# RWKV A products on the 64 rows of one head, the two heads by turns

## The chip, the core and the metric

The kernel runs on one core of a Trainium2 chip. A core has five engines with an instruction queue each: TensorE (PE in the profile, its weight loads PEld), VectorE (DVE), ScalarE (ACT), GpSimd (POOL) and SyncE (SP). Each queue runs in order, and semaphores make one queue wait for another. The metric is the device time of one execution in microseconds (us), lower is better; before, it is 991.96, the median of three runs.

## The reference

One step of a one-layer model: RWKV-7 time mixing and a differential attention on the same normalised input, gates, and an MLP. 512 prompt tokens and 64 sample tokens (8 sequences of 8) run together as 576 columns. The change lies in the RWKV part, eight heads of 64 channels:

```python
def rwkv7_scan(S0, r, w, k, v, a, b):
    ...
    def step(S, inp):
        r_t, w_t, k_t, v_t, a_t, b_t = inp
        sa = jnp.einsum('bhij,bhj->bhi', S, a_t)
        S = S * w_t[:, :, None, :] + sa[..., None] * b_t[:, :, None, :] + v_t[..., None] * k_t[:, :, None, :]
        return S, jnp.einsum('bhij,bhj->bhi', S, r_t)
...
    S, y = rwkv7_scan(S0, hs(r), hs(decay), hs(k), hs(v), -kk, kk * hs(a))
```

## The kernel before

**Chunks.** The scan is computed in nine chunks of 64 tokens, eight of the prompt and one of the samples (chunk 8). Within a chunk the steps become matrix products and a triangular inverse. The eight heads are handled as four pairs, `hp` 0 to 3; a pair fills the 128 partitions, head `par` 0 in rows 0 to 63, head `par` 1 in rows 64 to 127.

**`rwkv(hp)`** is a generator that prepares a pair, in stages that end at each `yield`. The first stage makes the tiles of keys and queries: `KB` has on the rows of each head, for each chunk, 64 columns of `b` and 64 of `k`; `ST0` and `ST1`, one for each head, have on the rows of their own head 64 columns of `a` and 64 of `r`, and zeros on the other 64 rows, put there by a memset on GpSimd (line 819). Then come the products called `pA`: for each head and each chunk `KB` (128 x 128) against that head's `ST` (128 x 128), with sums over 128 rows, of which 64 are zero. Groups of 4, 4 and 1 chunks write one PSUM bank each, named by pair, head and first chunk: `pA108` is pair 1, head 0, chunk 8. VectorE evicts a bank in two halves with a mask: the head's own rows of the result go to `ABR`, the other rows go into the zero half of `ST`, where they serve as the second operand of the scan.

The second stage transposes the values (`pV`, evicted by ScalarE into `SVU`) and `KB` (`pK`, into `KBt`), and multiplies the states of the samples with `ST` on 64 x 64 corners, the heads by turns (`pI`, copied by ScalarE into chunk 8 of `ST`). The third stage inverts the triangular part: ScalarE copies four pieces of 32 rows of `ABR`, two of each head, into `DT`; VectorE makes `Y` and the transposed `X` of it; TensorE multiplies 32 x 32 blocks (`pW`, `pZ`), in several rounds.

**`chain(pr)`** runs the scan over the chunks for two pairs at once, with the short products `pch`.

**Work beside it.** The projections of the input through the weights are the bulk of the work: `stream` yields one 128 x 128 by 128 x 288 product after another (`psz`, `psg` by name `ps_z`, `ps_g`; `gg` and `tz` are their evictions), and `take(n)` and `fill(n)` put n of them between the steps of the RWKV part. The calls `run(0, 0)`, `take(221)`, `run(0, 1, 1)` and so on at the end set in which order the stages of the pairs are written.

**What sets the order.** The tile framework's scheduler turns this into one queue for each engine, by priorities and by its own estimate of when an operand is ready; projections have the lowest priority (`FILL`), weight loads and evictions the highest (`FEED`). The order is fixed when the kernel is built. `bank(...)` gives one of three PSUM banks, which `pA`, `pV`, `pK`, `pI` and others share by turns; a bank is given anew when its evictions have ended. All products are in f32 with fp32r halves for the projections; helper `mm` is line 72, `tr` line 76, `act` line 58, `tt` line 61, so the profile's rows are told apart by their tiles.

Of the kernel before, what the change touches and what calls it, by code (L numbers as in the profile page):

```python
# [15 lines left out]
P = 128  # L16
# [20 lines left out]
C_ID, C_OB, C_M, C_MS, C_LM, C_I32, C_HS, C_SEL, C_MB, C_CM, C_END = (  # L37
    0, 128, 256, 384, 512, 672, 704, 706, 738, 746, 748)
# [3 lines left out]
def tile_hybrid_step(ctx, tc, xT, xsT, ktab, vtab, s0T, ptab, w_in, vecs, w2a2, g2, lamv,  # L42
# [3 lines left out]
    PE, VE, AE, GE = nc.tensor, nc.vector, nc.scalar, nc.gpsimd  # L46
# [13 lines left out]
    def tt(out, a, b, op, eng=None):  # L60
        ins = (eng or VE).tensor_tensor(out=out, in0=a, in1=b, op=op)  # L61
        if eng is None:
            ring["tt"] = ins

    def stt(out, a, s, b, op0, op1):
        VE.scalar_tensor_tensor(out=out, in0=a, scalar=s, in1=b, op0=op0, op1=op1)
# [4 lines left out]
    def mm(out, lhsT, rhs, start=True, stop=True):  # L71
        ring["mm"] = PE.matmul(out=out, lhsT=lhsT, rhs=rhs, start=start, stop=stop)  # L72
        return ring["mm"]
# [27 lines left out]
    def bank(name):  # L101
        return psw.tile([P, 512], F32, tag="w", name=name)
# [616 lines left out]
    def ch(a):  # L719
        return a.rearrange("p (c t) -> p c t", t=64)  # L720

    def m3(ap_, n):
        q, w = ap_.shape
        return ap_.rearrange("p (o w) -> p o w", o=1).broadcast_to([q, n, w])
# [15 lines left out]
    halves = [(par, slice(64 * par, 64 * par + 64)) for par in range(2)]  # L740

    def rwkv(hp):
        e = hp % 2
        own = pair.setdefault(hp // 2, {})
# [17 lines left out]
        nb = rt.tile([P, 5, P], F32, tag="G", name=f"nb{hp}", bufs=3)  # L762
# [50 lines left out]
        ST = []  # L813
        for par, rows in halves:
            stt(KB[rows, :, par], ch(aa)[rows], 0.5, ch(pinv)[rows], MUL, MUL)
            tt(KB[rows, :, 1 - par], ch(k2)[rows], ch(pinv)[rows], MUL)
            st = rb_.tile([P, NCH, 2, 64], F32, tag=f"ST{par}", name=f"ST{par}_{hp}")
            with tc.issue_after(own["nb"].ins) if hp == 0 else nullcontext():
                GE.memset(st[64 - 64 * par:128 - 64 * par], 0.0)
            stt(st[rows, :, 0], ch(kk)[rows], -1.0, ch(pm)[rows], MUL, MUL)  # L820
            tt(st[rows, :, 1], ch(r)[rows], ch(pe)[rows], MUL)
            ST.append(st)
        KBc = [KB[:, ci].rearrange("p a t -> p (a t)") for ci in range(NCH)]


        ABR = rb_.tile([P, NCH, 2, 64], F32, tag="ABR", name=f"ABR{hp}")
        for par in range(2):
            rows = slice(64 * par, 64 * par + 64)
            oth = slice(64 - 64 * par, 128 - 64 * par)
            for c0, cn, mk in ((0, 4, C_M), (4, 4, C_M), (8, 1, C_MS)):  # L830
                pA = bank(f"pA{hp}{par}{c0}")
                for i in range(cn):
                    mm(pA[:, i * P:(i + 1) * P], KBc[c0 + i], ST[par][:, c0 + i])
                pAv = pA[:, :cn * P].rearrange("p (c w) -> p c w", c=cn)
                f2 = lambda a: a[:, c0:c0 + cn].rearrange("p c a t -> p c (a t)")
                tt(f2(ABR)[rows], pAv[rows], m3(c[rows, mk:mk + P], cn), MUL)
                tt(f2(ST[par])[oth], pAv[oth], m3(c[oth, mk:mk + P], cn), MUL)
# [29 lines left out]
        for par in range(2):  # L867
            rows = slice(64 * par, 64 * par + 64)
# [202 lines left out]


    gens = [rwkv(hp) for hp in range(4)]

    def run(*stages):
# [249 lines left out]
    rows = []  # L1325
# [10 lines left out]
    for t0, n in LAST:  # L1336
# [63 lines left out]
        for d in range(KT):  # L1400
# [4 lines left out]
            if d + 1 in ends:  # L1405
                i = ends.index(d + 1)
# [119 lines left out]
```

## Time and profile before

| | |
|---|---|
| time, median of 3 runs (lowest, highest) | 991.96 us (991.02, 992.61) |
| profiled execution: time, span | 993.35 us, 991.6 us |
| mean granted TensorE clock | 0.989 |
| busy TensorE, its weight loads, VectorE, ScalarE, GpSimd | 97%, 92%, 70%, 50%, 9% |

The span runs from the first instruction to the last. Busy time by stretch, in us, with the granted clock:

| stretch | what is in it | TensorE | VectorE | ScalarE | clock |
|---|---|---|---|---|---|
| 180 to 206 | pair 0: `pA` to `pI` | 24.19 | 23.59 | 11.06 | 1.00 |
| 206 to 262 | pair 0: inverse; pair 1: tiles | 55.40 | 36.24 | 23.93 | 0.97 |
| 262 to 285 | pair 1: `pA` to inverse | 21.38 | 18.14 | 10.36 | 0.93 |
| 285 to 350 | scan of pairs 0 and 1; pair 2: tiles | 62.85 | 40.78 | 27.20 | 1.00 |
| 350 to 380 | pair 2: `pA` on; pair 3: tiles | 28.82 | 24.57 | 16.91 | 0.94 |
| 380 to 420 | pair 3: `pA` to inverse | 38.52 | 26.37 | 19.43 | 1.00 |
| 420 to 500 | scan of pairs 2 and 3, gates | 76.79 | 45.11 | 31.59 | 1.00 |
| 500 to 991.6 | output projections and MLP | 481.96 | 352.75 | 247.08 | 0.99 |

A row of a group of instructions gives line, engine, operation, output tile <- input tiles, the rows and columns of the array in use (128\*128), the tile's shape and type and the count; then busy time in us, mean ns of one, and the idle time just before them with what ended most of it. In rows in order of time, the first two numbers are start and duration in us, and square brackets hold a wait ahead of the row and what ended it. A product in f32 leaves two records.

### The profile page before, as it was taken

To read this page: it belongs to the slowest core of one execution; us is meant where nothing else is said; L and a number is where in the kernel's file an instruction comes from. 1 tells how busy PE (TensorE), PEld (TensorE's weight loads), DVE (VectorE), ACT (ScalarE), POOL (GpSimd) and SP (SyncE) were. 2 spreads that over 40 slices of the span, in tenths; PEclk is the share of its full clock that TensorE was granted. 3 is DMA by queue.
4 is the path that set the end of the run, shared out by engine and by line. 5 is a ranking of instruction groups with operands and counts; after the bars stand their busy time and mean duration, and the time that the engine had idled before them with its cause. 6 is when DMAs were issued, how large, how long until landed. Compare 5 with 4: busy or idle time off the path is not lost.

```text
span 991.6 us, 24377 instructions
## 1 busy us (share of the span) xinstructions
PE 964.5 (97%) x9996; PEld 913.4 (92%) x9996; DVE 694.3 (70%) x1459; ACT 495.1 (50%) x1084; POOL 91.0 (9%) x171
## 2 busy tenths in 40 slices
PE   8999999999999998999999999999999999999996
PEld 8999989898986898988889999999999999999996
DVE  6698566874945779445688898966666666666744
ACT  6576455354344455443344767444444444444732
POOL 2611100401003230001200000000000000000001
PEclk9999999999999999999999999999999999999998
DMA  7322673221112215222377642222222222221402
GB/s 266 128 76 76 210 220 117 80 59 52 44 63 74 79 62 161 79 70 100 121 234 223 209 132 97 87 94 86 86 86 86 85 86 86 86 87 42 136 3 95
DMA packets 50832, 105.73 MB, mean 107 GB/s; under 512 B 6066, under 2 KB 8114, under 8 KB 50594
## 3 DMA queue, kind: packets, MB, share of 16 engines
q1 hardware_dynamic: 47442, 96.95, 30.4%
q0 software_dynamic: 1648, 5.35, 1.5%
q8 instruction: 78, 1.28, 0.6%
q10 hardware_dynamic: 1632, 1.89, 0.5%
q14 instruction: 32, 0.26, 0.1%
HBM read 89.38 MB, written 14.78 MB: 105 GB/s over the span
## 4 chain that ended last, share of the span: by engine, by line
PE 83%; DVE 6%; issue 6%; ACT 3%; POOL 1%; DMA 0%; SPq 0%; DVEq 0%; POOLq 0%; ACTq 0%
PE ps_dn L72 21%; PE ps_z L72 8%; PE ps_g L72 7%; PE ux L1250 5%; PE ua L1250 5%; PE ps_wo L72 4%; PE ps_brb L72 3%; PE ps_k L72 3%; PE ub L1250 3%; PE ud L1250 3%; PE ps_bra L72 3%; PE uc L1250 3%; PE pch L1010 2%; PE ps_q L72 2%; PE ps_v L72 2%
## 5 line engine op out<-in xcount | busy, mean ns | idle before, releaser
L72 PE MATMUL ps_dn<-q,hi_dn 128*128 128x288 f32 x768 | 154.7, 296 | 0.0
L72 PEld LDWEIGHTS ps_dn<-q,hi_dn 128*128 128x128 f32 x768 | 122.9, 188 | 1.4
L72 PE MATMUL ps_dn<-q,lo_dn 128*128 128x288 f32 x384 | 113.3, 295 | 0.0
L72 PE MATMUL ps_g<-xl,hi_g 128*128 128x288 f32 x256 | 79.7, 311 | 0.0
L72 PE MATMUL ps_g<-xh,lo_g 128*128 128x288 f32 x256 | 79.2, 309 | 0.0
L72 PE MATMUL ps_g<-xh,hi_g 128*128 128x288 f32 x256 | 78.5, 307 | 0.0
L72 PEld LDWEIGHTS ps_dn<-q,lo_dn 128*128 128x128 f32 x384 | 72.2, 188 | 0.0
L72 PE MATMUL ps_z<-xh,lo_z 128*128 128x288 f32 (+1 forms) x224 | 69.2, 310 | 0.0
L72 PE MATMUL ps_z<-xh,hi_z 128*128 128x288 f32 (+1 forms) x224 | 68.0, 303 | 0.0
L72 PE MATMUL ps_z<-xl,hi_z 128*128 128x288 f32 (+1 forms) x224 | 66.9, 299 | 0.0
L61 DVE TENSOR_TENSOR ya<-ya,ps_dn 128x288 f32<-128x288 f32 x96 | 43.3, 451 | 27.6 <-PE ps_dn L72 27.5
L58 ACT ACTIVATE hi_dn<-raw_dn 128x512 fp32r<-128x512 f32 x48 | 30.1, 628 | 56.2 <-PE ps_dn L72 56.1
L58 ACT ACTIVATE c<-c 128x288 f32<-128x288 f32 x112 | 48.8, 440 | 9.4 <-DVE c L61 7.7
L1250 PE MATMUL ux<-h_t,hi 128*128 128x288 f32 x256 | 52.4, 297 | 0.0
L1250 PE MATMUL ua<-h_b,hi 128*128 128x288 f32 x256 | 52.2, 296 | 0.0
L72 PEld LDWEIGHTS ps_g<-xl,hi_g 128*128 128x128 f32 x256 | 48.9, 191 | 1.5
L72 PEld LDWEIGHTS ps_g<-xh,lo_g 128*128 128x128 f32 x256 | 49.0, 191 | 1.3
L72 PEld LDWEIGHTS ps_g<-xh,hi_g 128*128 128x128 f32 x256 | 48.8, 191 | 1.0
L58 ACT ACTIVATE hi<-a 128x1024 fp32r<-128x1024 f32 (+1 forms) x32 | 27.1, 846 | 43.1 <-PE ps_dn L72 34.9
L61 DVE TENSOR_TENSOR lo<-s,hi 128x1024 fp32r<-128x1024 f32 x32 | 39.2, 1224 | 10.4 <-ACT hi L58 10.3
L72 PE MATMUL ps_dn<-q,w 128*128 128x320 f32 (+1 forms) x336 | 46.3, 298 | 0.0
L72 PEld LDWEIGHTS ps_dn<-q,w 128*128 128x128 f32 x336 | 45.3, 190 | 0.1
(391 smaller groups left out, 2789.1 us busy)
## 6 DMA issues: line engine op xcount, KB each, us to landing
a<-in_w_up_dram SPq DMA_DIRECT2D x32, 512.0 KB, 3.3
raw_dn<-in_w_down_dram SPq DMA_DIRECT2D x64, 256.0 KB, 2.8
raw_g<-in_w_in_dram SPq DMA_DIRECT2D x32, 256.0 KB, 3.0
raw_z<-in_w_in_dram SPq DMA_DIRECT2D x28, 256.0 KB, 3.1
gt_d<-gg SPq DMA_DIRECT2D x16, 288.0 KB, 2.3
g<-gt_d SPq DMA_DIRECT2D x16, 288.0 KB, 3.6
kp<-in_ktab_dram SPq DMA_DIRECT2D x16, 256.0 KB, 4.0
vp<-in_vtab_dram SPq DMA_DIRECT2D x16, 256.0 KB, 3.4
```

What stands on the lines that cost most here:

```text
L58: ring["act"] = AE.activation(out=out, in_=in_, func=func, **kw)
L61: ins = (eng or VE).tensor_tensor(out=out, in0=a, in1=b, op=op)
L72: ring["mm"] = PE.matmul(out=out, lhsT=lhsT, rhs=rhs, start=start, stop=stop)
L1010: ring["mm"] = PE.matmul(out=ps[rows, e], lhsT=lhs, rhs=rhs, start=first and e == 1, stop=True, skip_group_check=True)
L1250: ring["mm"] = PE.matmul(out=ps[:, :288], lhsT=l[:, k], rhs=hb[blk][:, h, k], start=start and i == 0, stop=i == 11, skip_group_check=skip)
```

## The change

The products use only the rows of their head: `KB` and `ST` are cut to `[rows]`, 64 of the 128 rows of the array. The loop over the groups of chunks is now outside the loop over the heads: for each group two banks are taken, one for each head, and the products of the two heads are written by turns, one from the one half of the array's rows, the next from the other. Then both banks are evicted. The memset of the other half goes away; the evictions write there before anything reads it.

```diff
--- before.py
+++ after.py
@@ -815,8 +815,6 @@
             stt(KB[rows, :, par], ch(aa)[rows], 0.5, ch(pinv)[rows], MUL, MUL)
             tt(KB[rows, :, 1 - par], ch(k2)[rows], ch(pinv)[rows], MUL)
             st = rb_.tile([P, NCH, 2, 64], F32, tag=f"ST{par}", name=f"ST{par}_{hp}")
-            with tc.issue_after(own["nb"].ins) if hp == 0 else nullcontext():
-                GE.memset(st[64 - 64 * par:128 - 64 * par], 0.0)
             stt(st[rows, :, 0], ch(kk)[rows], -1.0, ch(pm)[rows], MUL, MUL)
             tt(st[rows, :, 1], ch(r)[rows], ch(pe)[rows], MUL)
             ST.append(st)
@@ -824,13 +822,16 @@
 
 
         ABR = rb_.tile([P, NCH, 2, 64], F32, tag="ABR", name=f"ABR{hp}")
-        for par in range(2):
-            rows = slice(64 * par, 64 * par + 64)
-            oth = slice(64 - 64 * par, 128 - 64 * par)
-            for c0, cn, mk in ((0, 4, C_M), (4, 4, C_M), (8, 1, C_MS)):
+        for c0, cn, mk in ((0, 4, C_M), (4, 4, C_M), (8, 1, C_MS)):
+            pAs = []
+            for par in range(2):
                 pA = bank(f"pA{hp}{par}{c0}")
-                for i in range(cn):
-                    mm(pA[:, i * P:(i + 1) * P], KBc[c0 + i], ST[par][:, c0 + i])
+                pAs.append(pA)
+            for i in range(cn):
+                for (par, rows), pA in zip(halves, pAs):
+                    mm(pA[:, i * P:(i + 1) * P], KBc[c0 + i][rows], ST[par][rows, c0 + i])
+            for (par, rows), pA in zip(halves, pAs):
+                oth = halves[1 - par][1]
                 pAv = pA[:, :cn * P].rearrange("p (c w) -> p c w", c=cn)
                 f2 = lambda a: a[:, c0:c0 + cn].rearrange("p c a t -> p c (a t)")
                 tt(f2(ABR)[rows], pAv[rows], m3(c[rows, mk:mk + P], cn), MUL)
```

`halves` is the list of (`par`, `rows`) of both heads.

On TensorE, around pair 0's products (`ps_z9` is a projection). Before:

```order
L72 MATMUL ps_z9_0_3032<-xl_104,hi_z9_1_3028 128x288
L72 MATMUL pA000_2825<-ST0_0_2814,KB0_2810 128x128 x4
L72 MATMUL pA004_2832<-ST0_0_2814,KB0_2810 128x128 x4
L72 MATMUL pA008_2839<-ST0_0_2814,KB0_2810 128x128
L72 MATMUL ps_z9_0_3032<-xh_103,lo_z9_1_3029 128x288
L72 MATMUL ps_z9_0_3032<-xh_103,hi_z9_1_3028 128x288
L72 MATMUL ps_z9_0_3032<-xl_104,hi_z9_1_3028 128x288
L72 MATMUL ps_z9_0_3032<-xh_103,lo_z9_1_3029 128x288
L72 MATMUL pA010_2843<-ST1_0_2820,KB0_2810 128x128 x4
L72 MATMUL ps_z9_0_3032<-xh_103,hi_z9_1_3028 128x288
```

and in the changed kernel:

```order
L72 MATMUL ps_z9_0_3030<-xl_104,hi_z9_1_3026 128x288
L72 MATMUL pA010_2824<-ST1_0_2819,KB0_2810 128x128 x4
L72 MATMUL pA004_2837<-ST0_0_2814,KB0_2810 128x128 x2
L72 MATMUL pA014_2838<-ST1_0_2819,KB0_2810 128x128 x2
L72 MATMUL pA004_2837<-ST0_0_2814,KB0_2810 128x128
L72 MATMUL pA014_2838<-ST1_0_2819,KB0_2810 128x128
L72 MATMUL pA004_2837<-ST0_0_2814,KB0_2810 128x128
L72 MATMUL pA014_2838<-ST1_0_2819,KB0_2810 128x128
L72 MATMUL pA008_2851<-ST0_0_2814,KB0_2810 128x128
L72 MATMUL ps_z9_0_3030<-xh_103,lo_z9_1_3027 128x288
```

The groups of 4 of the two heads now stand next to each other; head 1's first four stand before everything of the second group, whose rows alternate by twos and ones (head 0's first four stand further up, head 1's last further down, both between projections).

On TensorE around pair 1's first groups (`ps_z11`, `ps_g8` are projections). Before:

```order
L72 MATMUL ps_z11_1_3994<-xh_103,lo_z11_1_3990 128x296
L72 MATMUL pA104_3847<-ST0_1_3829,KB1_3825 128x128 x4
L72 MATMUL ps_g8_0_4064<-xh_103,hi_g8_0_4056 128x288
L72 MATMUL ps_g8_0_4064<-xl_104,hi_g8_0_4056 128x288
L72 MATMUL ps_g8_0_4064<-xh_103,lo_g8_0_4057 128x288
L72 MATMUL pA108_3854<-ST0_1_3829,KB1_3825 128x128
L72 MATMUL ps_g8_0_4064<-xh_103,hi_g8_0_4056 128x288
L72 MATMUL ps_g8_0_4064<-xl_104,hi_g8_0_4056 128x288
L72 MATMUL ps_g8_0_4064<-xh_103,lo_g8_0_4057 128x288
L72 MATMUL ps_g8_0_4064<-xh_103,hi_g8_0_4056 128x288
```

and in the changed kernel:

```order
L72 MATMUL ps_z11_1_3990<-xh_103,lo_z11_1_3986 128x296
L72 MATMUL pA110_3837<-ST1_1_3832,KB1_3823 128x128 x4
L72 MATMUL ps_g8_0_4060<-xh_103,hi_g8_0_4052 128x288
L72 MATMUL ps_g8_0_4060<-xl_104,hi_g8_0_4052 128x288
L72 MATMUL ps_g8_0_4060<-xh_103,lo_g8_0_4053 128x288
L72 MATMUL pA104_3850<-ST0_1_3827,KB1_3823 128x128 x4
L72 MATMUL ps_g8_0_4060<-xh_103,hi_g8_0_4052 128x288
L72 MATMUL ps_g8_0_4060<-xl_104,hi_g8_0_4052 128x288
L72 MATMUL ps_g8_0_4060<-xh_103,lo_g8_0_4053 128x288
L72 MATMUL ps_g8_0_4060<-xh_103,hi_g8_0_4052 128x288
```

Before, the three groups of head 0 stood first, those of head 1 fourteen rows later; now head 1's first group comes second. Each group of pair 1 still stands between projections.

On ScalarE in pair 1, from the copies into `DT` to those from `pI` and, in the changed kernel, the first round of the inverse (`W1_1`); `gg8` and `tz11` are evictions of projections. Before:

```order
L58 ACTIVATE DT1_4095<-ABR1_3839 32x288 x2
L58 ACTIVATE SVU0_2861<-pV1_0_3876 64x4x64 x2
L58 ACTIVATE gg8_4051<-gg8_4051 128x288
L58 ACTIVATE SVU0_2861<-pV1_0_3876 64x4x64 x2
L58 ACTIVATE DT1_4095<-ABR1_3839 32x288
L58 ACTIVATE SVU0_2861<-pV1_448_3885 64x64 x2
L58 ACTIVATE DT1_4095<-ABR1_3839 32x288
L58 ACTIVATE KBt1_3889<-pK10_3890 128x512
L58 ACTIVATE KBt1_3889<-pK14_3896 128x512
L58 ACTIVATE KBt1_3889<-pK18_3902 128x128
L58 ACTIVATE tz11_4045<-Z11_3979,vec_73 128x585
L58 ACTIVATE ST0_1_3829<-pI1_3915 64x64 x2
```

and in the changed kernel:

```order
L58 ACTIVATE gg8_4047<-gg8_4047 128x288
L58 ACTIVATE SVU0_2859<-pV1_0_3872 64x4x64 x4
L58 ACTIVATE SVU0_2859<-pV1_448_3881 64x64 x2
L58 ACTIVATE DT1_4091<-ABR1_3835 32x288
L58 ACTIVATE KBt1_3885<-pK10_3886 128x512
L58 ACTIVATE KBt1_3885<-pK14_3892 128x512
L58 ACTIVATE KBt1_3885<-pK18_3898 128x128
L58 ACTIVATE tz11_4041<-Z11_3975,vec_73 128x585
L58 ACTIVATE ST0_1_3827<-pI1_3911 64x64 x2
L58 ACTIVATE ST1_1_3832<-pI1_3911 64x64 x2
L58 ACTIVATE DT1_4091<-ABR1_3835 32x288 x3
L58 ACTIVATE W1_1_4104<-pW11_4105 128x288
```

The four copies into `DT` stood apart, all of them ahead of the copies from `pI`; now one stands ahead of them and three behind.

## The prediction

> **What bounds the kernel now.** I read the page first: the busy times and the chain that ended last.
>
> ```profile
> PE 964.5 (97%) x9996; PEld 913.4 (92%) x9996; DVE 694.3 (70%) x1459; ACT 495.1 (50%) x1084; POOL 91.0 (9%) x171
> PE 83%; DVE 6%; issue 6%; ACT 3%; POOL 1%; DMA 0%; SPq 0%; DVEq 0%; POOLq 0%; ACTq 0%
> ```
>
> TensorE is the bound: 97% busy, 83% of the chain. Its queue runs in the order written, so a microsecond that TensorE loses anywhere is lost at the end, unless it was about to wait there anyway. Then the groups of instructions, shapes kept apart:
>
> ```profile
> L72 PE MATMUL pA<-ST,KB 128*128 128x128 f32 x144 | 19.2, 280 | 0.3
> L61 DVE TENSOR_TENSOR ABR<-pA,cst_sb 64x512 f32<-64x512 f32 x16 | 11.0, 685 | 0.9 <-PE pA L72 0.6
> L819 POOL MEMSET ST<- 64x1152 f32 x8 | 8.4, 1056 | 24.1 <-PE pch L1010 23.8
> ```
>
> The 72 A products leave 144 records, two for each product in f32. A bank of four products is evicted by two VectorE instructions of 0.69 us. The eight memsets go away; GpSimd is 9% busy and no TensorE row names the memset as what it waited for, so I count their 8.4 us as nothing. What could lose that cover is VectorE's write of the next `ST`, which waits for the same buffer with or without them.
>
> **The price of a product now.** The order of time on TensorE where the first head pair's products stand:
>
> ```profile
> 194.72 2.23 PE L72 MATMUL pA<-ST,KB 128*128 128x128 f32 x18
> 196.70 0.38 PE L72 MATMUL ps_z<-xh,lo_z 128*128 128x288 f32 x1
> 196.92 0.29 PE L72 MATMUL ps_z<-xh,hi_z 128*128 128x288 f32 x1
> 197.05 0.30 PE L72 MATMUL ps_z<-xl,hi_z 128*128 128x288 f32 x1
> ```
>
> Eighteen records take 196.70 - 194.72 = 1.98 us: 0.11 a record, 0.22 a product, 72 x 0.22 = 15.9 us in all. The projections beside them follow one another every 0.13 us.
>
> **What a 64-row product can gain.** No row shows 64 rows by 128 columns in two halves by turns. The nearest is `pI`, two heads by turns on 64x64 corners:
>
> ```profile
> 205.24 1.11 PE L72 MATMUL pI<-ST,s 64*64 64x16 f32 x32 [0.35 <-ACT KBt L58]
> 206.28 0.41 PE L72 MATMUL ps_z<-xh,hi_z 128*128 128x296 f32 x1
> ```
>
> 32 records in 1.04 us are 0.033 each, well under the 0.11 of `pA` and, with half the columns, under half of that (0.055). So I take it that two records in different halves run side by side, and that each change of head between neighbouring products hides one record, 0.11 us (from 0 to 0.22, a whole product).
>
> But the products do not stand by turns. In the order of the changed kernel, which the scheduler makes, a head's four products are placed as soon as its own rows are ready. Pair 0 reads 4 | 4, 2, 2, 1, 1, 1, 1, 1 | 1 with projections at the bars: 7 changes of head. Pairs 2 and 3 have the same 7, pair 1 has none, as each of its six groups stands alone. 21 changes x 0.11 = 2.3 us, not the half of 15.9.
>
> **What a 64-row product costs.** One transpose in the trace has the new shape, 64 rows and 128 columns, among full-array work:
>
> ```profile
> 34.02 0.29 PE L72 MATMUL ps_q<-xl,hi_q 128*128 128x288 f32 x1
> 34.24 0.27 PE L76 MATMUL pb_R<-cst_sb,r 64*128 64x64 f32 x1
> 34.44 0.40 PE L72 MATMUL ps_q<-xh,lo_q 128*128 128x288 f32 x1
> 34.67 0.29 PE L72 MATMUL ps_q<-xh,hi_q 128*128 128x288 f32 x1
> 34.80 0.29 PE L72 MATMUL ps_q<-xl,hi_q 128*128 128x288 f32 x1
> ```
>
> From 34.02 to 34.67 stand 0.65 us for work that takes 0.13 + 0.11 + 0.13 = 0.37 at the usual spacing. So going into the shape and out again costs 0.28 us. The 128-row `pA` pays at most 0.09: the projection behind it takes 196.92 - 196.70 = 0.22 where 0.13 is usual; I leave that standing in both. I take 0.28 a group (0 if it were peculiar to the transpose, 0.4 if both ends were dearer). Groups that pay it anew: 3 in pair 0, 6 in pair 1, 3 in pair 2 (its first is cut in two by `pch`, which paid once already), 2 in pair 3 (between `pW` records). The Trainium skill, "TensorEngine Tiling (Array Packing)", Key Properties, says that a change of tiling mode, unlike a change of tile, drains the engine, which speaks against this change. Read strictly it charges changes between two small shapes too, as I do; charging only those to and from the full array, by the row alone, would take four round trips, 1.1 us, off the 14.
>
> **Banks.** `pA`'s pool has three banks. Before, a head's three groups filled them one after the other. Now groups 0 and 4 of both heads want four, and group 8 follows at once. Group 8's first product waits for both evictions of head 1's group 0: hand-over 0.3 + 2 x 0.69 + 0.15 = 1.8 us after that group ends, while the eight products between last 8 x 0.22 - 6 x 0.11 = 1.1. That gives a wait of 0.6 in pairs 0, 2 and 3, with all later projections queued behind it; it gives back most of what the overlap saved. In pair 2 the second product of group 8 waits again, about 0.5, because VectorE's queue now has a reduce and a gate eviction ahead of the evictions it needs. Waits of 0.1 to 0.2 that were there before go.
>
> **The copies behind it.** This is the largest term. Before, `ABR`'s rows of head 0 were complete while head 1's products still ran, so ScalarE copied two of the four `DT` pieces in idle time. Now both heads end together, and in ScalarE's queue for pair 1 three `DT` copies stand behind the `ST` copies from `pI`. ScalarE before:
>
> ```profile
> 268.07 0.90 ACT L58 ACTIVATE DT<-ABR 32x288 f32<-32x288 f32 x2 [3.79 <-DVE ABR L61]
> 270.48 0.77 ACT L58 ACTIVATE SVU<-pV 64x256 f32<-64x256 f32 x2 [1.51 <-PE pV L76]
> 271.26 0.44 ACT L58 ACTIVATE gg<-gg 128x288 f32<-128x288 f32 x1
> 271.72 0.77 ACT L58 ACTIVATE SVU<-pV 64x256 f32<-64x256 f32 x2
> 272.51 0.44 ACT L58 ACTIVATE DT<-ABR 32x288 f32<-32x288 f32 x1
> 272.86 0.43 ACT L58 ACTIVATE SVU<-pV 64x64 f32<-64x64 f32 x2
> 273.32 0.44 ACT L58 ACTIVATE DT<-ABR 32x288 f32<-32x288 f32 x1
> 273.78 1.25 ACT L58 ACTIVATE KBt<-pK 128x512 f32<-128x512 f32 x3
> 275.06 0.78 ACT L58 ACTIVATE tz<-Z,vec 128x585 f32<-128x585 f32 x1
> 275.75 0.65 ACT L58 ACTIVATE ST<-pI 64x64 f32<-64x64 f32 x4
> ```
>
> VectorE turns `DT` into `X`, and TensorE, which has nothing between `pI` and `pW` in either order, waits for `X`:
>
> ```profile
> 270.42 0.46 DVE L61 TENSOR_TENSOR gg<-ps_g,R 128x288 f32<-128x288 f32 x1
> ...
> 273.79 0.46 DVE L61 TENSOR_TENSOR Y<-DT,cst_sb 128x288 f32<-128x288 f32 x1 [0.69 <-ACT DT L58]
> ...
> 275.27 0.47 DVE L886 STREAM_TRANSPOSE X<-Y 128x288 f32<-128x288 f32 x1
> ```
>
> ```profile
> 269.60 0.29 PE L72 MATMUL ps_g<-xh,lo_g 128*128 128x288 f32 x1
> ...
> 274.43 1.11 PE L72 MATMUL pI<-ST,s 64*64 64x16 f32 x32 [0.68 <-ACT KBt L58]
> 275.80 0.82 PE L72 MATMUL pW<-X,DM 32*32 32x32 f32 x72 [0.26 <-DVE X L886]
> ```
>
> In the new order ScalarE's run begins with `gg`, which needs the half of `ps_g` that ended at 269.60 + 0.29 = 269.89. The same products and projections stand ahead of it, plus six round trips: 269.89 + 6 x 0.28 = 271.6. VectorE's `gg` takes 0.46, so ScalarE starts near 272.0. Then without a pause, by starts of the rows above: gg 0.46, four SVU 1.58, two SVU 0.46, DT 0.46, KBt 1.28, tz 0.69, ST 0.65, three DT 1.35, together 6.9: 278.9. `Y` to the end of `X` is 275.74 - 273.79 = 1.95: 280.9. `pW` starts there instead of at 275.80, 5.1 us later. Were the drains free, ScalarE would still start no earlier than the 271.26 of its `gg` now, and `pW` would be 4.4 late. With 0.4 a drain it would be 5.8. I take 5.0. TensorE stands still for some 4 us of it with the whole rest of the kernel queued behind. In pairs 0 and 2 over 90 projections stand between `pI` and `pW`, some 12 us, so the same late copies are covered there.
>
> **The sum** (us): pair 0: 3 x 0.28 - 7 x 0.11 + 0.6 - 0.2 = +0.4. Pair 1: +5.0. Pair 2: 0.84 - 0.77 + 0.6 + 0.5 - 0.2 = +1.0. Pair 3: 0.56 - 0.77 + 0.6 = +0.4, less part of these two pauses, as its evictions end earlier now and the `pch` products come later, among others of their kind:
>
> ```profile
> 392.29 0.63 PE L76 MATMUL pV<-cst_sb,P 128*128 128x128 f32 x4 [0.32 <-DVE ST L61]
> 393.77 0.34 PE L1010 MATMUL pch<-SVU,ST 128*64 128x64 f32 x4 [0.85 <-ACT SVU L58]
> ```
>
> Of 0.32 + 0.85 I take 0.8 (0 to 1.2): -0.4. Together +6.0. The profiled execution has a span of 991.6 and a time of 993.35, so it should become 997.6 and 999.4; it lies 1.4 above the median of the runs, 991.96, which becomes 998.0.
>
> **Rivals.** *Full pairing, not slower.* If weight loads of the other half were pulled ahead over runs of four, every pair of products would cost one, and drains vanish in it: 4.0 us of a head pair become 2.0. Pairs 0, 2 and 3 give -6.0, pair 1 stays at +4.4, as ScalarE's run does not depend on it: 990.4. It decides once pairing saves over 4.4 of the 6.0. For it speaks `pI`'s 0.033; against it the order, and banks that must be emptied first. The Trainium skill, "TensorEngine Tiling (Array Packing)", Theoretical Speedup, allows up to twofold for a contraction of 64 or less, which is this case; no run here shows it. Chance 0.06.
>
> *The copies cost nothing*, if ScalarE came to them earlier than its queue suggests: pair 1 costs its drains alone, 1.7, the sum is +2.7, 994.7. Against it: ScalarE runs in order too. Chance 0.10.
>
> *Drains are free* for these products: 8 x 0.28 less outside pair 1, 0.6 less in it: 995.2. Chance 0.08. *No overlap at all*: +2.3, of which the bank waits absorb half: 999.2. Chance 0.10.
>
> *The clock.* In the stretch that begins just behind pair 1's `pW` and the short products of the scan, TensorE is granted half its clock for 3.41 us (the columns are the window and its length, the busy times of TensorE, its weight loads, VectorE, ScalarE and GpSimd, the granted clock, the DMA share and GB/s):
>
> ```profile
> 277.35:280.76 3.41, 3.41 (x82) 3.07 (x82) 1.77 (x4) 0.63 (x1) 0.00 (x0) 0.50 0.08 15
> ```
>
> The new pause covers this window itself; another may follow it, or one arise in pair 3, where `pA` now stands among `pW`. Each costs up to 3.41 / 2 = 1.7: 999.7. Chance 0.16.
>
> The forecast itself has 0.50. A measurement of this kernel can tell 0.2%, 2.0 us, from no change. Faster by more than that: 0.03, from full pairing. Within it: 0.03 of full pairing, half of the copies' rival and some of the drains' tail, 0.10. Slower: 0.87. The range from 994.6 to 1000.2 leaves out full pairing and the tails of the others.
>
> **What would show it.** Right: `pA` as 64*128; no `ps_` record within 0.13 of a group's ends; `pW` of pair 1 waiting some 4 us for VectorE's `X`, with three `DT` behind `ST<-pI` on ScalarE; 21 places where records of different heads start nearly together. Wrong: `pW` of pair 1 less than 3 us late, records of one head closer than 0.11, or a loss in the stretch after 500 us, which nothing here touches.

## The result and the profile after

| | before | changed |
|---|---|---|
| time, median of 4 runs (lowest, highest) | 991.97 us (991.02, 992.61) | 1001.21 us (998.88, 1001.91) |
| ratio, 95% interval | | 1.009 (1.007 to 1.0109) |
| profiled execution: time, span | 993.35, 991.6 us | 1001.91, 999.8 us |

The change makes the kernel slower by 9.2 us. The direction was forecast; the size was not: 998.0 was forecast, with 1000.2 as the upper end. The page of the changed kernel, and its row for the products:

```profile
PE 965.3 (97%) x9996; PEld 910.5 (91%) x9996; DVE 693.5 (69%) x1459; ACT 495.0 (50%) x1084; POOL 81.7 (8%) x163
```

```profile
L72 PE MATMUL pA<-ST,KB 64*128 64x128 f32 x144 | 18.8, 291 | 1.6 <-DVE ST L61 1.6
```

TensorE is as busy as before in a longer span, on 64 rows now, and waits 1.6 us for banks. Where the 8.2 us of span arose is read from lags: the start of a product in one trace less the start of the same product (the same place in its group's count) in the trace of before. This table has them for the changed kernel and for the experiments below, in us; the numbers in brackets are those of the experiments. Executions differ by up to 1.1 us before the first `pA`, so differences between rows count, not the rows.

| start in before, us | what | changed | rows (1) | turns (2) | DT (3) | strict (4) | scan late (5) | scan early (6) | two (7) | one (8) | both (9) | rows, scan (10) |
|---|---|---|---|---|---|---|---|---|---|---|---|---|
| 192.05 | ahead of pair 0's `pA` | 0.03 | -0.37 | -0.24 | -0.47 | -1.04 | 0.03 | -0.44 | -0.94 | -1.00 | -0.42 | -0.52 |
| 230.21 | pair 0's inverse | 0.60 | 0.38 | -0.52 | 0.83 | -0.49 | 0.06 | 0.18 | -0.26 | -1.51 | 0.87 | 0.24 |
| 252.89 | pair 1's tiles | 0.28 | -0.17 | -1.87 | 0.31 | -1.84 | -0.42 | -1.18 | 0.31 | -1.94 | 0.48 | -1.12 |
| 260.35 | ahead of pair 1's `pA` | 0.67 | 0.21 | -1.49 | 0.68 | -1.47 | -0.40 | -0.81 | 0.17 | -1.57 | 0.86 | -0.74 |
| 274.43 | pair 1's `pI` | 2.19 | 1.72 | -1.81 | 3.53 | -0.85 | -0.39 | 0.71 | 1.88 | -6.01 | 3.73 | 0.77 |
| 276.04 | pair 1's `pW` | 6.19 | 1.72 | 2.19 | 3.20 | 3.16 | -0.39 | 4.71 | 1.55 | -1.71 | 3.40 | 0.76 |
| 296.69 | its inverse's end | 6.96 | 0.50 | 2.98 | 2.53 | 2.89 | -0.37 | 5.51 | 1.75 | -1.56 | 2.17 | -0.44 |
| 360.30 | pair 2's `pI` | 7.85 | 1.35 | 2.92 | 3.43 | 3.06 | -0.36 | 6.39 | 2.69 | -1.55 | 3.03 | 0.40 |
| 380.04 | ahead of pair 3's `pA` | 7.85 | 1.35 | 2.92 | 3.42 | 1.54 | -0.37 | 6.38 | 2.68 | -1.56 | 3.03 | 0.41 |
| 419.05 | pair 3's inverse | 7.20 | 1.82 | 3.89 | 2.75 | 5.75 | 1.05 | 6.33 | 3.30 | -0.54 | 3.09 | 0.28 |
| 443.43 | `pg`, ahead of the second scan | 7.30 | 2.17 | 3.51 | 2.29 | 5.82 | -0.16 | 6.20 | 3.27 | -0.22 | 2.09 | 0.22 |
| 458.54 | in the second scan | 8.35 | 3.23 | 4.58 | 3.36 | 6.88 | -0.14 | 6.10 | 4.34 | -0.21 | 2.01 | 0.13 |
| 881.43 | MLP | 8.49 | 3.32 | 4.37 | 3.10 | 6.58 | 1.55 | 5.63 | 3.94 | -0.19 | 1.72 | 0.06 |

**Pair 0.** TensorE in order of time (start, duration, engine, line, output <- inputs, count, the wait ahead in brackets):

```profile
196.52 2.10 PE L72 MATMUL pA<-ST,KB 64*128 64x128 f32 x24
199.25 0.46 PE L72 MATMUL pA<-ST,KB 64*128 64x128 f32 x2 [0.63 <-DVE ST L61]
```

24 records with the seven changes of head start within 2.10 - 0.27 = 1.83 us (0.27 is the length of the last record). One behind the other they would take 22 x 0.112 + 0.213 = 2.68, 0.213 for the first and 0.112 for each further one, as the spacing in groups of one head is: 0.85 saved, 0.12 for each change. Then chunk 8's product waits 0.63 for its bank.

**Pair 1.** ScalarE, then VectorE's way to `X`, then TensorE:

```profile
273.10 0.44 ACT L58 ACTIVATE gg<-gg 128x288 f32<-128x288 f32 x1 [8.14 <-DVE gg L61]
273.58 2.04 ACT L58 ACTIVATE SVU<-pV 64x256 f32<-64x256 f32 x6
275.52 0.43 ACT L58 ACTIVATE DT<-ABR 32x288 f32<-32x288 f32 x1
275.98 1.25 ACT L58 ACTIVATE KBt<-pK 128x512 f32<-128x512 f32 x3
277.10 0.80 ACT L58 ACTIVATE tz<-Z,vec 128x585 f32<-128x585 f32 x1
277.78 0.67 ACT L58 ACTIVATE ST<-pI 64x64 f32<-64x64 f32 x4
278.46 1.34 ACT L58 ACTIVATE DT<-ABR 32x288 f32<-32x288 f32 x3
```

```profile
279.83 0.46 DVE L61 TENSOR_TENSOR Y<-DT,cst_sb 128x288 f32<-128x288 f32 x1 [0.82 <-ACT DT L58]
...
281.31 0.47 DVE L887 STREAM_TRANSPOSE X<-Y 128x288 f32<-128x288 f32 x1
```

```profile
276.62 1.11 PE L72 MATMUL pI<-ST,s 64*64 64x16 f32 x32
281.84 1.18 PE L72 MATMUL pW<-X,DM 32*32 32x32 f32 x72 [4.11 <-DVE X L887]
```

ScalarE runs from 273.10 to 279.80 without a pause; the last three `DT` copies stand behind the copies from `pI`, `X` ends at 281.78, and TensorE waits 4.11 us for it.

**The second scan.** Here the changed kernel loses 1.05 us (7.30 to 8.35) that the forecast does not have. Before, and then changed:

```profile
446.07 1.14 PE L72 MATMUL pg<-P,wg 128*128 128x288 f32 x4
447.14 1.15 PE L1010 MATMUL pch<-SVU,ST 128*64 128x64 f32 x32
448.22 0.53 PE L72 MATMUL ps_brb<-obh,hi_brb 128*128 128x288 f32 x2
```

```profile
453.21 0.75 PE L72 MATMUL pg<-P,wg 128*128 128x288 f32 x2
454.29 0.75 PE L72 MATMUL pg<-P,wg 128*128 128x288 f32 x2 [0.33 <-ACT oa L58]
454.97 0.33 PE L1011 MATMUL pch<-SVU,ST 128*64 128x64 f32 x2
455.23 0.40 PE L72 MATMUL ps_brb<-obh,lo_brb 128*128 128x288 f32 x1
...
456.62 1.15 PE L1011 MATMUL pch<-SVU,ST 128*64 128x64 f32 x30
```

Before, six of the first eight products of this scan (16 records) stood in pair 3's pauses, from 393.77 on, and two at 439.70. Now all eight stand at 446.98, where the two stood, and behind them the queue is ordered otherwise. The lag is still 7.30 ahead of `pg` and is lost in the lines shown: `pg`, cut by a wait for `oa`, takes 454.97 - 453.21 = 1.76 us to what follows it, for 447.14 - 446.07 = 1.07 before, and one of the next small products (two records) stands alone between projections.

### The profile page after: what moved, and what is told of

It reads as the page before. It is cut to its first block, busy times and chain, and to the rows that moved or that the text cites. A ratio compares the mean times of both kernels' runs of the same rounds, so it can differ in the third digit from the quotient of the medians.

```text
span 999.8 us, 24364 instructions
## 1 busy us (share of the span) xinstructions
PE 965.3 (97%) x9996; PEld 910.5 (91%) x9996; DVE 693.5 (69%) x1459; ACT 495.0 (50%) x1084; POOL 81.7 (8%) x163
## 4 chain that ended last, share of the span: by engine, by line
PE 56%; DVE 1%; ACT 1%; issue 0%; POOL 0%; DVEq 0%
PE ps_dn L72 21%; PE ux L1251 5%; PE ua L1251 5%; PE ps_g L72 5%; PE ps_wo L72 4%; PE ub L1251 3%; PE ud L1251 3%; PE uc L1251 3%; PE ps_brb L72 3%; PE ps_bra L72 3%; PE pch L1011 1%; PE pZ L72 0%; PE pW L72 0%; PE pg L72 0%; ACT oa L58 0%
```

## Experiments

**1 and 2: the rows or the order.** The first has the loops of before with 64-row operands and no memset, the second the loops and the order of the changed kernel with 128-row operands and zeros.

```diff
-            with tc.issue_after(own["nb"].ins) if hp == 0 else nullcontext():
-                GE.memset(st[64 - 64 * par:128 - 64 * par], 0.0)
...
-                    mm(pA[:, i * P:(i + 1) * P], KBc[c0 + i], ST[par][:, c0 + i])
+                    mm(pA[:, i * P:(i + 1) * P], KBc[c0 + i][rows], ST[par][rows, c0 + i])
```

> The loops of the kernel before (one head after the other), with the operands cut to 64 rows and without the memset. Theory 1 (the loss has two causes: entering and leaving the 64-row shape, 0.39 us a group by the changed kernel's own rows, and the order): pair 1's five groups start as before and each costs 0.39 more, pW of pair 1 waits under 0.7 us for X, no products of two heads are neighbours and none overlap; 11 to 13 groups x 0.39 = +4.3 to +5.1, less up to 1.0 of waits ahead of pA that the longer way covers: 995 to 997. Theory 2 (the order alone costs, the 64-row form costs nothing outside it): 991.5 to 993. Theory 3 (the 64-row form is the whole loss): 1000 to 1002.

Measured: 995.25, ratio 1.0031 (1.002 to 1.0042).

```diff
+            with tc.issue_after(own["nb"].ins) if hp == 0 else nullcontext():
+                GE.memset(st[64 - 64 * par:128 - 64 * par], 0.0)
...
-                    mm(pA[:, i * P:(i + 1) * P], KBc[c0 + i][rows], ST[par][rows, c0 + i])
+                    mm(pA[:, i * P:(i + 1) * P], KBc[c0 + i], ST[par][:, c0 + i])
```

> The loops and the order of the changed kernel, but 128-row operands with zero halves and the memset. Theory 1: no 0.39 us a group and no overlap of two heads (records of pA 0.11 apart throughout); the waits for a bank ahead of chunk 8's products in pairs 0 and 2 are there, 0.5 to 1 us each, and pW of pair 1 waits 3.5 to 4.5 us for X: +5 to +7, 997 to 999. Theory 2 (order alone): 1000 to 1002. Theory 3 (64-row form alone): 991.5 to 993.

Measured: 998.40, ratio 1.0065 (1.0052 to 1.0079). Both came as the first theory had it. Neither alone is the loss: in parts of a thousand of the time it is 3.1 and 6.5, which add to 9.6, and the changed kernel has 9.0. In the first, pair 1 has the order of before, and the same group of one product (two records) between projections can be compared. Before, then 64 rows:

```profile
264.56 0.30 PE L72 MATMUL ps_g<-xh,lo_g 128*128 128x288 f32 x1
264.69 0.39 PE L72 MATMUL pA<-ST,KB 128*128 128x128 f32 x2
264.83 0.38 PE L72 MATMUL ps_g<-xh,hi_g 128*128 128x288 f32 x1
265.05 0.29 PE L72 MATMUL ps_g<-xl,hi_g 128*128 128x288 f32 x1
```

```profile
265.24 0.29 PE L72 MATMUL ps_g<-xh,lo_g 128*128 128x288 f32 x1
265.46 0.48 PE L72 MATMUL pA<-ST,KB 64*128 64x128 f32 x2
265.88 0.40 PE L72 MATMUL ps_g<-xh,hi_g 128*128 128x288 f32 x1
266.12 0.30 PE L72 MATMUL ps_g<-xl,hi_g 128*128 128x288 f32 x1
...
276.15 1.11 PE L72 MATMUL pI<-ST,s 64*64 64x16 f32 x32 [0.69 <-ACT KBt L58]
277.52 0.82 PE L72 MATMUL pW<-X,DM 32*32 32x32 f32 x72 [0.26 <-DVE X L884]
```

265.05 - 264.56 = 0.49 and 266.12 - 265.24 = 0.88: a group in the 64-row shape costs 0.39 us more among full-array work; a group of four products in pair 1 costs as much more, 1.55 for 1.16. With the old order `pW` waits 0.26 for `X`, as before. The second has the wait for `X` (the row says what waited, for whom, us in all, times, the longest), and its 26 records in pair 0 start within 3.22 - 0.27 = 2.95 us, 0.12 each: full rows by turns do not overlap.

```profile
PE pW L72 <- DVE X L889: 4.1, 1, 4.1
```

```profile
195.83 3.22 PE L72 MATMUL pA<-ST,KB 128*128 128x128 f32 x26
```

**3: the late copies.** The four copies into `DT` are written at the end of the first stage of `rwkv`.

```diff
...
+        DT = rt.tile([P, NCH, 32], F32, tag="DT", name=f"DT{hp}")
+        for g in range(4):
+            gs = slice(32 * g, 32 * g + 32)
+            act(DT[gs], ABR[gs, :, 0, 32 * (g % 2):32 * (g % 2) + 32])
         yield
...
```

> The changed kernel with the four copies into DT written at the end of the first stage, so that they stand ahead of KBt and the copies from pI in ScalarE's queue. If the late copies are what pW of pair 1 waits for: that wait of 4.1 us falls under 1 us and the time falls by 3 to 4 us, to 997 to 998. If something else would have kept TensorE there (KBt, or VectorE's queue), the wait changes its name and the time stays at 1000 to 1002.

Measured: 998.12, ratio 1.0064 (1.005 to 1.0079). ScalarE and TensorE in pair 1:

```profile
273.44 1.78 ACT L58 ACTIVATE DT<-ABR 32x288 f32<-32x288 f32 x4
275.25 2.04 ACT L58 ACTIVATE SVU<-pV 64x256 f32<-64x256 f32 x6
```

```profile
276.16 0.69 PE L1011 MATMUL pch<-SVU,ST 128*64 128x64 f32 x16 [1.28 <-ACT SVU L58]
...
277.96 1.11 PE L72 MATMUL pI<-ST,s 64*64 64x16 f32 x32 [0.29 <-ACT KBt L58]
279.00 0.82 PE L72 MATMUL pW<-X,DM 32*32 32x32 f32 x72
```

`pW` waits no more; of the 4.1 us 1.3 come back as a wait for `SVU`, whose evictions now stand behind the `DT` copies. `pW` lags 3.20 in place of 6.19. So the copies were the cause of that wait.

**4: strict turns.** Each group of four is chained so that the heads alternate.

```diff
+            lead = None
             for i in range(cn):
-                for (par, rows), pA in zip(halves, pAs):
-                    mm(pA[:, i * P:(i + 1) * P], KBc[c0 + i][rows], ST[par][rows, c0 + i])
+                for par, rows in reversed(halves):
+                    with tc.issue_after(lead.ins) if lead else nullcontext():
+                        lead = mm(pAs[par][:, i * P:(i + 1) * P], KBc[c0 + i][rows], ST[par][rows, c0 + i])
```

> The changed kernel with the products of a group chained on TensorE so that the heads truly alternate in each group of four. Theory 1 (each change of head hides one record of 0.11 us): some 58 changes of head in place of 21, -4.1 us; about two 0.39 us entries fewer, -0.8; the single product of the next group that now stands behind a group waits for its bank in pairs 0 and 2, +0 to +3; the late DT copies stay: 996 to 1000. A group of four products of each head takes 8 x 0.11 + 0.11 = 1.0 us and not 1.8. If two halves overlap only at a change of runs and not steadily: no gain from the order, 1000 to 1003.

Measured: 1001.11, ratio 1.0097 (1.0079 to 1.0114). The time is that of the second alternative, but not for its reason. Its first group and its waits:

```profile
195.10 1.38 PE L72 MATMUL pA<-ST,KB 64*128 64x128 f32 x18
```

```profile
PE pA L72 <- DVE ST L61: 4.6, 5, 2.9
```

The overlap is there: 18 records start within 1.38 - 0.27 = 1.11 us, where the row of before has 1.95. The wait of 4.1 us for `X` is there as well, and 4.6 us are waited for banks, 2.9 of them at once in pair 3 (at 391.40). Ahead of the evictions that this product waits for, VectorE's queue has `y`, which itself waits for GpSimd:

```profile
389.20 0.76 DVE L61 TENSOR_TENSOR y<-y,var 128x576 f32<-128x576 f32 x1 [1.69 <-POOL var L243]
389.87 0.68 DVE L61 TENSOR_TENSOR ABR<-pA,cst_sb 64x512 f32<-64x512 f32 x1
390.56 0.69 DVE L61 TENSOR_TENSOR ST<-pA,cst_sb 64x512 f32<-64x512 f32 x1
```

So much of that wait is the order of VectorE's queue; in the other four waits, 1.7 us together, VectorE is busy throughout. Behind the long wait TensorE has half its clock for 10.24 us, and the lag grows from 1.54 to 5.75 in pair 3.

**7, 8 and 12: the overlap with fewer groups or more banks**, and `DT` early. The seventh has two groups a pair, in three banks:

```diff
+        for run_ in (((0, 4, C_M, (1, 0)), (8, 1, C_MS, (1,))), ((4, 4, C_M, (1, 0)), (8, 1, C_MS, (0,)))):
...
```

> 64-row operands in two groups a pair: first four chunks of both heads by turns and chunk 8 of head 1, then the other four by turns and chunk 8 of head 0; DT copied early. A pair's products take 8 x 0.11 + 0.22 twice and one odd product, 2.5 us, with three entries of 0.39 3.6 us against 4.0 and up to 0.6 of waits in the kernel before: -0.5 in pairs 0 and 2, +0.5 in pair 1 (its waits are given back), no wait of 4 us for X, +1.06 in the second scan, 0 to +2 in pair 3: 992.5 to 995.5. If the waits for banks eat the overlap as in the strict turns: 996 to 999.

Measured: 997.03, ratio 1.005 (1.0032 to 1.0067): the second alternative, with 2.9 us of waits for banks. The eighth has one group of all 18 products in pairs 0 and 1, with the scan's two banks and the inverse's bank beside the three; pairs 2 and 3 are those of before.

```diff
+        if hp < 2:
+            more = {(0, 0): lambda n: tbank(n), (0, 1): lambda n: cbank(0, n), (4, 1): lambda n: cbank(1, n)}
...
```

> Pairs 0 and 1 with 64-row operands, all 18 products in one group, by turns, into six banks (the scan's and the inverse's banks are free there), DT copied early; pairs 2 and 3 as in the kernel before. A pair's products take 18 x 0.11 + 0.39 = 2.4 us against 4.0, in pair 1 0.6 more as its first product stands alone. If TensorE keeps what it gains: -1.6 and -1.0, less up to 1 where pV waits for a bank: 989.5 to 991.5. If VectorE, which evicts at the same pace, sets the end of these stages: the gain is waited away ahead of pbn and X, 991.5 to 993.

Measured: 992.03, ratio 1.0007 (0.9995 to 1.0019): no difference that can be told. TensorE in pair 0:

```profile
195.15 2.28 PE L72 MATMUL pA<-ST,KB 64*128 64x128 f32 x36
197.35 0.77 PE L76 MATMUL pV<-cst_sb,P 128*128 128x128 f32 x5
...
199.77 0.65 PE L76 MATMUL pK<-cst_sb,KB 128*128 128x128 f32 x4 [0.42 <-ACT SVU L58]
...
201.92 0.66 PE L76 MATMUL pK<-cst_sb,KB 128*128 128x128 f32 x4 [1.36 <-DVE ST L61]
```

36 records start within 2.01 us, 0.057 each: the two halves run side by side throughout, at twice the rate of before. The 1.6 us gained (2.4 for 4.0) are then waited for at `pK`, which needs a bank that VectorE, busy throughout, has not emptied; the lag falls by only 0.51. This is what the Trainium skill says in "TensorEngine Tiling (Array Packing)", PSUM Bottleneck: tiling speeds up the array and not the evacuation. The twelfth adds twelve projections to pair 1's stage, to cover a wait for `DM`:

```diff
-    take(106)
+    take(118)
...
-    take(190)
+    take(178)
```

> As the one-group kernel, with twelve projections moved from pair 2's stage into pair 1's between pI and pW, where TensorE waited 1.5 us for VectorE's DM. If that wait only lacked work to cover it: 12 x 0.13 = 1.6 us less, 990 to 991, ahead of the kernel before. If VectorE's queue sets the end of that stage, the wait moves on to W and DM of the next rounds: 991.5 to 992.5.

Measured: 992.89, ratio 0.9999 (0.9986 to 1.0012). In its trace the wait falls from 1.5 to 0.5 and the span to 989.9, 1.5 less than the eighth's, but the medians do not show it (992.84 for the kernel before beside it). The 1.5 need not come from the edit: the eighth's trace has a half-clock window of 3.41 us in pair 1's inverse, at 275.16, the twelfth's none. No version that beats the kernel before was found.

**5, 6, 10 and 9: the place of the second scan's first products.** The fifth puts them late in the kernel before, the sixth early in the changed kernel.

```diff
-            R = entry(*here[0])
+            with tc.issue_after(ring["mm"].ins) if pr and ci == 0 else nullcontext():
+                R = entry(*here[0])
```

> The kernel before, with the first eight products of the second scan (pch10, the entry of chunk 0) held behind the stage ahead of it, so that they stand at the scan and not in pair 3's pauses, as in the changed kernel. If their place is what the changed kernel loses in the second scan: the lag against the kernel before grows by 1.0 to 1.1 us between the pg products at 443 us and the projections at 458 us, and shrinks by up to 0.85 at 393 us, where they were waited for: in all +0.2 to +1.1, 992 to 993.5. If that loss has another cause: no lag grows there.

Measured: 995.13, ratio 1.0032 (1.0021 to 1.0044). Missed in place and size: no lag grows from 443 to 458 us, but 1.2 by 486 and 0.5 more by 497; it is 1.55 near the end of the trace, and by the ratio the kernel is 3.2 us slower. In the sixth, the priority at the start of the second stage is kept, for the second scan that of pair 3:

```diff
+        own["at"] = tc.cur_priority
...
+            with prio(own["at"]) if pr and ci == 0 else nullcontext():
+                R = entry(*here[0])
```

> The changed kernel, with the first eight products of the second scan given the priority of pair 3's second stage, so that they stand among pair 3's products again. If their place is the cause: the 1.06 us that the changed kernel loses between 443 and 458 us of the kernel before are gone, the rest of its lags stays: 999.5 to 1001. If not: 1001 as it was, with 1.06 still lost there.

Measured: 999.04, ratio 1.0081 (1.0064 to 1.0098). The place is as it was before:

```profile
452.28 1.14 PE L72 MATMUL pg<-P,wg 128*128 128x288 f32 x4
453.34 1.15 PE L1012 MATMUL pch<-SVU,ST 128*64 128x64 f32 x32
```

The lag shrinks by 0.10 where it grew by 1.05. The tenth does the same to the first experiment:

> The loops of the kernel before with 64-row operands, and the second scan's first products among pair 3's. If the 64-row form alone costs 0.39 us a group and the place of the scan's products was the other part of its +3.1: 995.25 - 1.06 = 994.2 (993 to 995). If the scan's place costs nothing there: 995.3.

Measured: 994.51, ratio 1.0018 (1.0007 to 1.0029), and again the 1.06 are gone (2.17 to 3.23 in the first, 0.22 to 0.13 in the tenth). The intervals of the ratios overlap in both pairs of runs; it is the lags that show it. So the place of these eight products costs 1 us in the changed kernel's order. In that of before, putting them late cost 1.5 in the trace, elsewhere. The ninth has both repairs:

> The changed kernel with both repairs: DT copied early and the second scan's first products among pair 3's. If these two places are the separate causes that the runs so far suggest, their gains add: 1001.2 - 3.1 - 1.1 = 997 (995.5 to 998), no wait of 4 us for X, no half clock of 6.83 us behind it, no 1.06 lost between 443 and 458 us; what is left, +3 to +5, is the 0.39 us a group and the waits for banks. If they share one cause: 998 to 999 as with DT alone.

Measured: 998.62, ratio 1.0058 (1.0042 to 1.0075). The time lies in the second alternative (one shared cause); but the kernel before took 992.84 beside it, and the ratio on 991.97 is 997.7, in the first. The trace has neither the wait of 4 us for `X` nor the loss of 1.05. In the ratios the repairs add (9.0 less 2.6 less 0.9 is 5.5), but the trace has a span of 993.3 and lags of 1.72 at the end: the other runs are slower than this trace.

**11: the memset back.**

```diff
+            with tc.issue_after(own["nb"].ins) if hp == 0 else nullcontext():
+                GE.memset(st[64 - 64 * par:128 - 64 * par], 0.0)
```

> The changed kernel with the memset of ST's other half put back (it is overwritten by the evictions). If GpSimd's time is free here, as forecast: 1000 to 1002, the lags within 0.2 us at the same places. If GpSimd's queue matters (its nb and vm are waited for by TensorE): 0.5 to 2 us more, in the waits of pk and pF.

Measured: 1000.64, ratio 1.008 (1.0065 to 1.0094). The memset's 8.4 us are worth nothing here: TensorE's waits for GpSimd are those of the changed kernel, 2.0 for `pk` and 1.5 for `pF`.

**Four more traces: the clock.** The third kernel once more, the ninth twice and the changed kernel once: single runs of 998.54, 998.21, 998.06 and 1000.36.

> The kernel with the early DT copies once more, for a second trace: its first trace had no half-clock window before the last 10 us and a span of 994.4, its other runs a mean clock of 0.990 to 0.993 and spans up to 998. If the windows are what makes the difference: a trace at 0.991 to 0.993 shows two or three windows of 3.41 us more, each some 1.0 to 1.7 us long in lost time where TensorE works from its queue, and lags of 3 to 4 us that begin in these windows. If the lag grows outside such windows, the clock isn't the cause.

> The kernel with both repairs, for a second trace: spans of 993.3 and 993.7 at a clock of 0.996, 996.7 to 998.0 at 0.991 to 0.993. Windows as the cause: the extra lag begins in half-clock windows, and these follow pairs 0 to 3's stretches of short products. Otherwise it grows where the clock is whole.

> The same kernel a third time, so that a trace of each sort can stand side by side; by the windows the difference of two spans is the sum of what the windows cost, by any other cause it isn't.

> The changed kernel again, for a second trace: its runs have spans of 996.9 to 1000.1. A half-clock window of 6.83 us behind pair 1's wait of 4 us, as in every trace with that wait so far; a span under 998 goes with fewer windows elsewhere, not with a shorter wait.

The ninth kernel's first trace, then its second, in three stretches of the same place (the columns are those of the prediction's window row):

```profile
275.66:279.07 3.41, 2.41 (x53) 2.05 (x53) 2.04 (x7) 3.28 (x9) 0.00 (x0) 1.00 0.02 5
279.07:282.48 3.41, 3.41 (x164) 3.13 (x161) 2.02 (x6) 2.07 (x8) 0.00 (x0) 1.00 0.02 5
282.48:285.90 3.42, 3.42 (x122) 3.05 (x121) 2.34 (x6) 1.39 (x3) 0.00 (x0) 1.00 0.28 81
```

```profile
275.66:279.07 3.41, 3.41 (x43) 2.96 (x45) 2.16 (x7) 3.05 (x8) 0.00 (x0) 0.50 0.02 5
279.07:282.48 3.41, 3.41 (x93) 3.31 (x92) 0.62 (x3) 1.07 (x5) 0.00 (x0) 0.50 0.02 5
282.48:285.90 3.42, 3.42 (x82) 3.08 (x82) 1.63 (x3) 0.63 (x1) 0.00 (x0) 0.50 0.14 52
```

The same kernel, with TensorE at full and at half clock: 339 records against 218. Against each other the two traces stand at -0.76 ahead of this place and at 2.63 behind it, 3.4 us for 10.24 us of half clock, and that is nearly all that their spans differ by (996.4 - 993.3 = 3.1). The third trace has 6.83 us there and loses 2.2 against the first (-0.07 ahead, 2.12 behind). Not all is the clock: 0.9 more of its lag, and 0.6 of the second trace's, arise at 419 to 443 us, where none of the three has such a window. The third kernel's second trace has a window of 3.41 us in pair 1's inverse and one in pair 3; its lag grows by 2.9 us more than in the first trace, 0.7 and 1.4 of it at these two places. So pair 1's inverse draws half-clock windows, none to three of 3.41 us, in one execution more than in another: in the traces of the changed kernel and of experiments 2, 3, 4, 6, 9 and 11 they are 5.3 us on average (11 traces), in the others 1.9 (7 traces). The changed kernel has 6.83 us in its own trace, where the lag grows by 0.77 (6.19 to 6.96), and 3.41 in its second, as the kernel before has, where it shrinks by 0.20 (5.22 to 5.02). I had thought that the wait of 4 us brings 6.83 us of them: the changed kernel's second trace has that wait and half of them, and the second and third traces of the ninth kernel have them without that wait.

## Why the forecast was right in kind and wrong in size

The terms, against the lags of the changed kernel's trace:

| term | forecast | trace |
|---|---|---|
| pair 0 | +0.4 | 0.60 - 0.03 = +0.6 |
| pair 1, start of `pW` | +5.0 | 6.19 - 0.67 = +5.5 |
| half clock in pair 1's inverse | 0 | 6.96 - 6.19 = +0.8 |
| pair 2 | +1.0 | 7.85 - 6.98 = +0.9 |
| pair 3 | -0.4 | 7.20 - 7.85 = -0.65 |
| second scan | 0 | 8.35 - 7.30 = +1.05 |

- *Copies behind it*: right in mechanism and nearly in size. ScalarE's run took 6.7 us (6.9 forecast) and `Y` to `X` 1.95; it began at 273.10 and not 272.0, since `gg` came later by the dearer entries and by a lag of 0.67 that was there already. The third experiment shows the cause.
- *Price of the shape*: mis-sized. 0.28 came from one transpose; a group costs 0.39, as the rows of the first experiment show. The rule of the Trainium skill in "TensorEngine Tiling (Array Packing)", Key Properties, that a change of tiling mode drains the engine, agrees with these rows. 14 groups would be 1.5 us more, but in pair 1 waits of before went into them: its six groups moved `pI` by 2.19 - 0.67 = 1.5 us, not 2.3.
- *Overlap*: right, 0.12 for each change of head against 0.11. Within runs of one head nothing overlaps (0.112 a record), so what the rival of full pairing asked for did not come in this order; steady turns do run at twice the rate (experiments 4 and 8).
- *Banks*: right in pair 0, 0.63 for 0.6. The fourth and eighth experiments show what full pairing would have met: the rival with 990.4 counted what TensorE saves and not when VectorE empties the banks.
- *Pair 3 and the scan*: this step failed. It counted the pauses ahead of `pV` and `pch` as won, because the `pch` products come later "among others of their kind". Moved there, they cost 1.05 in the second scan, a term that the sum puts at nothing; with the products back among pair 3's (experiments 6 and 10) that loss is gone.
- *Clock*: this term failed too. The sum has none, and the rival with 0.16 stands alone, not with others; 0.8 came in pair 1's inverse. Before had windows at 243, 277 and 363 us. Without the first and the third the changed kernel won 0.9 (1.18 to 0.29) and 1.2 us (7.84 to 6.62) at these places; ahead of the next pair's `pA` 0.4 and all of the 1.2 were lost again (0.28 to 0.67, 6.62 to 7.85), 1.1 of both as longer waits for VectorE at `pbn` (2.6 us for 1.5). In pair 1's inverse windows do cost, and in these traces they come more often with the changed order.
- *The memset at nothing*: right (experiment 11).
- *Pair 0*: its sum comes to 0.47 and stands in the forecast as 0.4; the trace has 0.6.

The trace came out 999.8 for 997.6 forecast: 1.05 the scan, 0.8 the clock, 0.5 pair 1. A stall of 0.6 at 232 to 237 us, which the profile puts down to nothing, is open. The median lies 3.2 above the forecast; the rest of that, 0.7, is that the profiled execution of before was 1.4 above its median and that of the changed kernel 0.7. The upper end of the range was too low since it had no term for the scan and let the rivals come only one at a time; the scan and the clock came together. How much of the clock comes differs by execution: the changed kernel's second trace, with one window less in pair 1's inverse, has a span of 998.6.

Open: what decides whether a half-clock window comes, why the fifth experiment loses 3.2 us by its ratio and 1.55 in its trace, and what the 0.9 us at 419 to 443 in the ninth kernel's traces are.

## What to carry to other kernels

A product on half the rows was not half the price where it stood alone: each visit to the shape cost a fixed time, paid by the group, so ask how many groups the scheduler makes of it, and whether the banks are emptied at the pace of the twofold rate. When a loop is turned so that two results end together and no longer one behind the other, look for the small copies that used to run between them. A product that leaves a pause has to be priced where it goes as well as where it was.

## What the runs showed of the hardware

A group on 64 x 128 between projections took 0.39 us more than on full rows, with 2 records (0.88 for 0.49) and with 8 (1.55 for 1.16). Two heads on the two row halves, by turns into different banks, ran at 0.057 us a record against 0.112 on full rows, steadily over 36 records. Half-clock windows came in steps of 3.41 us, and one execution of the same kernel had none where another had three, which lost 3.4 us, a third of their length. The Trainium skill, "TensorE: Matmul & The Clock Gate", What's actually happening, has the half rate after an idle window of some 3.4 us and the full rate after a busy one. The changed kernel's second trace agrees, with no product in the window ahead:

```profile
277.20:280.62 3.42, 0.00 (x0) 0.00 (x0) 2.60 (x8) 1.59 (x5) 0.00 (x0) 1.00 0.00 0
280.62:284.03 3.41, 3.16 (x80) 3.10 (x81) 0.61 (x2) 0.41 (x1) 0.00 (x0) 0.50 0.02 5
```

The three windows above do not: TensorE is busy throughout the first two, by the profile (which models the ends of products), and stays at half. Nor was the window ahead of them idle: it has 1.71 us of products. The measurement decides: a window busy by the profile did not end the half rate here.
